# Weight quadrants on the queue of GpSimd, and TensorE in program order within the gate and up products

## The chip, the cores and the metric

The kernel runs on one core of one Trainium2 chip. A core has TensorE (PE, the matrix engine), VectorE (DVE), ScalarE (ACT), GpSimd (POOL) and SyncE (SP). Each runs its own list of instructions in order and waits on semaphores where it needs another's result. SP, ACT and POOL can each put transfers on a queue of their own; 16 DMA engines carry them out. The metric is the time of one execution on the device in microseconds; a lower time is better.

## The reference

The reference is one step of a two-layer streaming encoder for 512 new frames (with 16 meta tokens in front) and 32 frames of a running stream, 560 columns in all. Each layer is a feed-forward half step, a mixer (gated linear attention in layer 0, latent attention in layer 1) and another feed-forward half step. Nearly all of what matters here is in the half steps, of which there are four:

```python
def swiglu_half(h, norm_w, w_gate, w_up, w_down):
    hn = rmsnorm(h, norm_w)
    return h + 0.5 * ((jax.nn.silu(hn @ w_gate) * (hn @ w_up)) @ w_down)
```

The model width is 1024 and the inner width 2816. All data are 32-bit floats.

## The kernel before, in words

**Numbers in two parts.** A matmul takes its operands as a high and a low part. `split` (L330) makes them: ACT casts the source to the high part (L331), DVE subtracts that from the source for the low part (L332). `mm` (L370) multiplies high by high (L378), low weight by high (L379) and high weight by low (L381).

**Seven products for eight.** The gate and up products of a half step treat the 1024 rows of a weight block and the 560 columns of the input as two halves each, and replace the eight block products by seven products of sums and differences (a Strassen scheme). For each pair `f` of 128-column blocks of the inner width, `quads` (L435) loads four quadrants of the weights, r11, r12, r21 and r22, into tiles named `fr` (six buffers), by `quadrant` (L354), two transfers of 256 KB each, gate and up. It forms sums of quadrants on DVE (L451) and hands out the seven weight operands in the order r11, r12, r11 + (r21 + r22), r21 + r22, r21 + r11, r22, and r12 plus the third; `whole` (L360) splits each into tiles `whi` and `wlo` (four buffers of each).

**The order of the seven.** `gate_up` (L467) runs them into three pairs of PSUM banks, A, B and C: b11 into A, b21 into C, t6 onto A, t5 into B, t7 onto A, t4 into C, b22 onto B. After each of them `between` may put in pieces of the down product of the group before (`down`, L544; output Y, added to `h` on DVE at L556). `finish` (L493) combines two banks, scales the columns by the norm's reciprocal root, and makes silu(gate) * up.

**The norm's roots** are not ready when a half step starts. `roots` (L402) has PE sum the squares across partitions (six small matmuls, L410), DVE take a reciprocal square root in eleven small steps (`rsqrt`, L422, lines 424 to 432), and, in the function `finish` that it returns, PE spread the result over the partitions (three transposes, L417). In the first `gate_up` of a half step the program has `roots(0)` between b21 and t6, the first use of its result (L417) after t5, then `roots(1)`, and its L417 behind t7. In the very first half step (`lazy`) `roots(0)` comes after t6.

**Stages.** `ffn` (L562) runs a half step: five groups of `f`, of 2, 4, 4, 4 and 8 blocks, each with its down product; that of the last group runs after the others, alone. In it, and in the last projection of a mixer, the input operands of the next half step are made, and the weights of its first two products are loaded ahead into tiles `raw` (`first_weights`, L348, with `quadrant` too). The other weights are loaded by `load` (L334, transfer at L341) into `raw` (two buffers).

**What sets the order.** A planner (the tile framework) sets the order of each engine's list: it walks through the program with a model of the costs and gives an engine, when it is free, the earliest instruction of the program that is ready in the model. So an engine's list may differ from the order in which the program names its instructions. A `manual_schedule` block holds the engines named to the order of the program for the instructions inside it; the others, and where the block's instructions fall among those outside, stay the planner's. Once set, an engine's list is followed in order on the chip, waits included; so are the queues. All weights are transferred by SP's queue.

Of the kernel before, what the change touches and what calls it, by code (L numbers as in the profile page):

```python
# [52 lines left out]
def weight_plan():  # L53
# [3 lines left out]
    def ffn(i, l):  # L57
        for gi, (f0, f1) in enumerate(GROUPS):
# [3 lines left out]
            for m in range(ND):  # L62
                plan.append((("d", i, l, gi, m), f1 - f0))

    ffn(1, 0)
    for h in range(GH):
        plan.extend((("v", h, j), nk * V_COLS[h] / P) for j, nk in enumerate(V_PARTS[h]))
# [4 lines left out]
        if h >= 2:  # L72
            plan.extend((("go", h - 2, c), 8) for c in range(4))
    ffn(2, 0)
    ffn(1, 1)
    for m in range(6):
        plan.append((("wd", m), 8))
# [212 lines left out]
class Net:  # L290
# [61 lines left out]
        return self.whole(raw)  # L352

    def quadrant(self, t, i, l, f, q):  # L354
        for j, x in enumerate("gu"):
            off, n = PLAN[x, i, l, f + q // 2]
            src = self.a["W"][off:off + P * n].rearrange("(p k c) -> p k c", p=P, k=2)[:, q % 2]
            self.nc.sync.dma_start(t[:, 512 * j:512 * j + 512], src)

    def whole(self, src):  # L360
        hi = self.w.tile([P, 8, P], F32R, name="whi", tag="whi")
# [200 lines left out]
    def ffn(self, i, l, xs, halves, side, turn):  # L562


        ap, fw = Pools(self.tc, side), Pools(self.tc, side)
        acp = ap(f"act{i}{l}")
        if xs.lazy:
            free = [acp.tile([P, 2, T // 2], F32, name="xt", tag=f"a{x}{j}") for j in range(4, 8) for x in "hl"]
            xs.tmp = [t[:, k, :] for t in free for k in range(2)]
        raws, tp = fw(f"raw{i}{l}", 6), fw(f"tmp{i}{l}", 1)  # L570
        fill = []
        last = len(GROUPS) - 1
        for gi, (f0, f1) in enumerate(GROUPS):
            j0 = 4 * (gi % 2) if gi < last else 0
            acts = [(acp.tile([P, T], F32R, name=f"ah{j}", tag=f"ah{j}"),
                     acp.tile([P, T], F32R, name=f"al{j}", tag=f"al{j}")) for j in range(j0, j0 + 4 if gi == last else j0 + f1 - f0)]
            slots = [7 * min((f1 - f0) // 2, 2) - 1]

            def between(k):
                if slots[0] <= 0 or (slots[0] == 7 * min((f1 - f0) // 2, 2) - 1 and k < 2):  # L580
                    return
                for _ in range(-(-len(fill) // slots[0])):
                    fill.pop(0)()
                slots[0] -= 1

            for f in range(f0, f1, 2):
                if gi == last and f == f0 + 4:
                    assert not fill
                    acts += [(acp.tile([P, T], F32R, name=f"ah{j}", tag=f"ah{j}"),
                              acp.tile([P, T], F32R, name=f"al{j}", tag=f"al{j}")) for j in range(4, 8)]  # L590
                self.gate_up(i, l, f, xs, acts[f - f0:f - f0 + 2], raws, tp, between)
            assert not fill
            order = [(m, hf) for m in range(ND) for hf in (0, 1)]
            if gi < last:
                fill = self.down(i, l, gi, acts, halves, order)
        fw.close()
        after = turn()
        order = Quads.ORDER if isinstance(after, Quads) else (
            [(0, 0), (1, 0), (0, 1), (1, 1), (2, 0), (3, 0), (2, 1), (3, 1)] + [(m, hf) for hf in (0, 1) for m in range(4, 8)])
        for f in self.down(i, l, last, acts, halves, order, after):  # L600
            f()
        ap.close()
# [967 lines left out]
```

## Time and profile before

| | us |
|---|---|
| median of three runs | 2117.19 |
| the three runs | 2110.93, 2117.34, 2117.19 |
| the profiled execution | 2109.41 |
| its span, first to last instruction | 2107.5 |
| PE busy | 2026.0 (96%) |
| DVE busy | 1643.2 (78%) |
| ACT busy | 1018.4 (48%) |
| POOL busy | 51.4 (2%) |

In the rows of the profile a group is named by line, engine, operation and output<-inputs, with the tile's shape; "x24" is a count, and a bracket at the end of a timeline's row holds the idle time of the engine before it and what ended that. PE's weight loads (PEld) run beside its matmuls. "SPq" is SP's queue: it issues transfers and waits, and has no busy time. The granted clock is the share of full speed at which PE was allowed to run. The four half steps begin, as PE sees it, at about 0, 679, 1070 and 1707 us.

### The profile page before, as it was taken

To read this page: it belongs to the slowest core of one execution; us is meant where nothing else is said; L and a number is where in the kernel's file an instruction comes from. 1 tells how busy PE (TensorE), PEld (TensorE's weight loads), DVE (VectorE), ACT (ScalarE), POOL (GpSimd) and SP (SyncE) were. 2 spreads that over 40 slices of the span, in tenths; PEclk is the share of its full clock that TensorE was granted. 3 is DMA by queue.
4 is the path that set the end of the run, shared out by engine and by line. 5 is a ranking of instruction groups with operands and counts; after the bars stand their busy time and mean duration, and the time that the engine had idled before them with its cause. 6 is when DMAs were issued, how large, how long until landed. Compare 5 with 4: busy or idle time off the path is not lost.

```text
span 2107.5 us, 38039 instructions
## 1 busy us (share of the span) xinstructions
PE 2026.0 (96%) x15290; PEld 1980.2 (94%) x15290; DVE 1643.2 (78%) x3097; ACT 1018.4 (48%) x1822; POOL 51.4 (2%) x117
## 2 busy tenths in 40 slices
PE   5999999999999899999989999999999979999997
PEld 5999999989999799999979999999988969999997
DVE  8887878556658888788778877886788788878884
ACT  6444445455445444445545444454575454444451
POOL 0000000101110000000000000000210000000000
PEclk8999999999999899999989999999999989999998
DMA  3323222222221332322222322222211223232221
GB/s 131 106 87 107 93 96 78 77 68 71 73 80 55 108 103 82 106 86 91 81 95 96 105 92 91 95 83 92 61 51 59 71 86 100 90 111 91 96 72 62
DMA packets 93633, 183.29 MB, mean 87 GB/s; under 512 B 10433, under 2 KB 22081, under 8 KB 93457
## 3 DMA queue, kind: packets, MB, share of 16 engines
q1 hardware_dynamic: 89632, 176.24, 26.1%
q10 hardware_dynamic: 3824, 4.63, 0.7%
q8 instruction: 120, 1.97, 0.4%
q14 instruction: 57, 0.46, 0.1%
HBM read 176.84 MB, written 3.99 MB: 86 GB/s over the span
## 4 chain that ended last, share of the span: by engine, by line
PE 82%; DVE 10%; ACT 3%; DMA 2%; issue 2%; SPq 0%; POOL 0%; DVEq 0%; ACTq 0%; POOLq 0%
PE Y L381 8%; PE Y L378 8%; PE Y L379 8%; PE A L379 5%; PE A L381 5%; PE A L378 5%; PE ps L378 4%; PE ps L381 4%; PE ps L379 4%; PE B L378 3%; PE B L379 3%; PE B L381 3%; PE C L379 3%; PE C L381 3%; PE C L378 3%; DVE wlo L332 3%
## 5 line engine op out<-in xcount | busy, mean ns | idle before, releaser
L332 DVE TENSOR_TENSOR wlo<-fr,whi 128x1024 fp32r<-128x1024 f32 x302 | 363.9, 1216 | 17.2 <-ACT whi L331 17.0
L378 PE MATMUL Y<-ah,whi 128*128 128x280 f32 (+1 forms) x1408 | 373.8, 291 | 1.9 <-ACT ah L331 1.0
L379 PE MATMUL Y<-ah,wlo 128*128 128x280 f32 (+1 forms) x1408 | 373.4, 292 | 0.0
L331 ACT CAST whi<-fr 128x1024 fp32r<-128x1024 f32 x302 | 313.3, 1049 | 92.9 <-PE C L381 34.6
L378 PE MATMUL A<-x,whi 128*128 128x280 f32 (+1 forms) x1056 | 286.3, 296 | 29.5 <-ACT whi L331 29.5
L379 PE MATMUL A<-x,wlo 128*128 128x280 f32 (+1 forms) x1056 | 285.7, 296 | 1.0 <-DVE wlo L332 1.0
L378 PEld LDWEIGHTS Y<-ah,whi 128*128 128x128 f32 x1408 | 265.2, 188 | 3.4 <-ACT ah L331 1.7
L556 DVE SCALAR_TENSOR_TENSOR h<-Y,h 128x280 f32<-128x280 f32 (+1 forms) x320 | 140.9, 443 | 161.9 <-PE Y L381 161.2
L379 PEld LDWEIGHTS Y<-ah,wlo 128*128 128x128 f32 x1408 | 265.4, 188 | 0.0
L332 DVE TENSOR_TENSOR wlo<-raw,whi 128x512 fp32r<-128x512 f32 (+5 forms) x237 | 203.6, 861 | 76.7 <-ACT whi L331 71.9
L331 ACT CAST whi<-raw 128x512 fp32r<-128x512 f32 (+5 forms) x237 | 176.0, 744 | 173.4 <-PE ps L381 55.2
L381 PE MATMUL Y<-al,whi 128*128 128x280 f32 (+1 forms) x1408 | 233.9, 292 | 0.0
L378 PEld LDWEIGHTS A<-x,whi 128*128 128x128 f32 x1056 | 203.9, 193 | 31.1 <-ACT whi L331 31.1
L451 DVE TENSOR_TENSOR fr<-fr 128x1024 f32<-128x1024 f32 x176 | 214.5, 1219 | 20.4 <-DMA fr<-W 18.1
L379 PEld LDWEIGHTS A<-x,wlo 128*128 128x128 f32 x1056 | 203.7, 193 | 1.7 <-DVE wlo L332 1.4
L381 PEld LDWEIGHTS Y<-al,whi 128*128 128x128 f32 x1408 | 201.2, 189 | 0.0
L378 PE MATMUL B<-x,whi 128*128 128x280 f32 (+1 forms) x704 | 188.6, 293 | 3.4 <-ACT whi L331 3.4
L379 PE MATMUL C<-x,wlo 128*128 128x280 f32 (+1 forms) x704 | 187.1, 292 | 3.5 <-DVE wlo L332 3.5
L379 PE MATMUL B<-x,wlo 128*128 128x280 f32 (+1 forms) x704 | 187.4, 292 | 0.8 <-DVE wlo L332 0.8
L378 PE MATMUL C<-x,whi 128*128 128x280 f32 (+1 forms) x704 | 187.4, 291 | 0.6 <-ACT whi L331 0.6
L381 PE MATMUL A<-x,whi 128*128 128x280 f32 (+1 forms) x1056 | 181.2, 294 | 0.0
L490 ACT COPY r<-A 128x560 f32<-128x560 f32 (+1 forms) x132 | 82.2, 623 | 174.1 <-PE A L381 173.8
(368 smaller groups left out, 4059.2 us busy)
## 6 DMA issues: line engine op xcount, KB each, us to landing
fr<-W SPq DMA_DIRECT2D x352, 256.0 KB, 3.4
raw<-W SPq DMA_DIRECT2D x80, 512.0 KB, 3.5
raw<-W SPq DMA_DIRECT2D x112, 256.0 KB, 2.9
raw<-W SPq DMA_DIRECT2D x40, 128.0 KB, 2.1
h<-xT SPq DMA_DIRECT2D x3, 560.0 KB, 7.6
raw<-W SPq DMA_DIRECT2D x4, 384.0 KB, 3.1
o_y<-h SPq DMA_DIRECT2D x8, 136.0 KB, 2.2
o_y<-h ACTq DMA_DIRECT2D x8, 136.0 KB, 1.9
```

Of the source, the lines that this page charges most:

```text
L331: self.nc.scalar.copy(hi, src)
L332: self.nc.vector.tensor_tensor(lo, src, hi.bitcast(F32), op=ALU.subtract)
L378: f(hi[:, b0 + k, :], xh[:, c], start=not more and k == 0, stop=False)
L379: f(lo[:, b0 + k, :], xh[:, c], start=False, stop=False)
L381: f(hi[:, b0 + k, :], xl[:, c], start=False, stop=k == n - 1)
L451: add = lambda out, x, y: nc.vector.tensor_tensor(out, x, y, op=ALU.add)
L490: nc.scalar.copy(r[:, :, :n], of[:, :, :n])
L556: nc.vector.scalar_tensor_tensor(self.h[:, m, c], Y[:, :n], 0.5, self.h[:, m, c], op0=ALU.mult, op1=ALU.add)
```

## The change

Two things change. `quadrant` puts its transfers on the queue of GpSimd, except those of the very first pair of blocks of the first half step, which stay on SP; this holds for the `fr` tiles and for the first weights of the later half steps, which go into `raw`. And every call of `gate_up` runs inside a block that holds PE to the order of the program. That block includes the pieces of the down product that `between` puts in, and the matmuls of the roots; the planner still sets the order of DVE, ACT, SP and POOL.

```diff
     def quadrant(self, t, i, l, f, q):
+
+        queue = self.nc.sync if (i, l, f) == (1, 0, 0) else self.nc.gpsimd
         for j, x in enumerate("gu"):
             off, n = PLAN[x, i, l, f + q // 2]
             src = self.a["W"][off:off + P * n].rearrange("(p k c) -> p k c", p=P, k=2)[:, q % 2]
-            self.nc.sync.dma_start(t[:, 512 * j:512 * j + 512], src)
+            queue.dma_start(t[:, 512 * j:512 * j + 512], src)
...
-                self.gate_up(i, l, f, xs, acts[f - f0:f - f0 + 2], raws, tp, between)
+                with self.tc.manual_schedule(engines={mybir.EngineType.PE}):
+                    self.gate_up(i, l, f, xs, acts[f - f0:f - f0 + 2], raws, tp, between)
```

## The prediction

> **What bounds the kernel now.** I read the page first, then the busy time by stretches, then the waits of PE, then the timelines around each place where PE stood still.
>
> The head of the page:
>
> ```profile
> span 2107.5 us, 38039 instructions
> PE 2026.0 (96%) x15290; PEld 1980.2 (94%) x15290; DVE 1643.2 (78%) x3097; ACT 1018.4 (48%) x1822; POOL 51.4 (2%) x117
> ```
>
> PE sets the time and has 81 us without work. The waits of PE (total, times, longest) say what ended most of them:
>
> ```profile
> PE A L378 <- ACT whi L331: 29.5, 6, 8.8
> PE Y L417 <- DVE ry L432: 21.4, 8, 3.3
> ```
>
> The view by stretches says where (stretch, length, busy time of PE, PEld, DVE, ACT and POOL with counts, granted clock, DMA share, GB/s):
>
> ```profile
> 0.00:58.00 58.00, 33.09 (x185) 30.72 (x186) 46.88 (x108) 36.62 (x76) 0.20 (x4) 0.85 0.39 128
> 58.00:333.60 275.60, 275.60 (x2141) 275.60 (x2140) 226.57 (x329) 127.44 (x196) 0.00 (x0) 1.00 0.30 97
> 679.00:703.00 24.00, 13.71 (x84) 12.78 (x83) 20.72 (x48) 9.59 (x15) 0.00 (x0) 0.72 0.43 137
> 703.00:775.00 72.00, 71.75 (x557) 71.52 (x556) 61.49 (x93) 35.40 (x58) 0.00 (x0) 1.00 0.31 98
> 1077.00:1095.50 18.50, 8.74 (x44) 7.80 (x43) 14.64 (x34) 5.53 (x8) 0.00 (x0) 0.63 0.19 60
> 1713.00:1734.00 21.00, 8.49 (x38) 7.56 (x38) 15.57 (x35) 6.69 (x9) 0.00 (x0) 0.59 0.53 163
> ```
>
> Inside a feed-forward stage PE has no gap (275.60 of 275.60), so no order of its work and no queue can make that part shorter. What is to be won lies at the four starts of such a stage: idle 24.9 (0 to 58), 10.3, 9.8 and 12.5 us, with the clock down to 0.59 to 0.85. The first start keeps its loads on SP. So the forecast is made at the other three. The second stage's start, on PE, DVE, ACT and SP (start, length, line, form, idle time before it):
>
> ```profile
> 685.12 0.72 PE L410 MATMUL Y<-ones,acc 128*128 128x1 f32 x6
> 688.73 0.54 PE L417 MATMUL Y<-ident,ry 128*128 128x128 f32 x3 [2.88 <-DVE ry L432]
> 689.11 1.19 PE L410 MATMUL Y<-ones,acc 128*128 128x1 f32 x6
> 693.59 0.87 PE L417 MATMUL Y<-ident,ry 128*128 128x128 f32 x3 [3.30 <-DVE ry L432]
> 698.23 0.60 PE L378 MATMUL A<-x,whi 128*128 128x280 f32 x1 [3.76 <-ACT whi L331]
> ...
> 688.51 0.16 DVE L432 SCALAR_TENSOR_TENSOR ry<-rt,ry 128x3 f32<-128x3 f32 x1
> 693.29 0.15 DVE L432 SCALAR_TENSOR_TENSOR ry<-rt,ry 128x3 f32<-128x3 f32 x1
> 693.37 4.99 DVE L451 TENSOR_TENSOR fr<-fr 128x1024 f32<-128x1024 f32 x4
> ...
> 697.13 1.99 ACT L331 CAST whi<-fr 128x1024 fp32r<-128x1024 f32 x2 [2.24 <-DVE fr L451]
> ...
> 679.10 0.80 SPq L358 DMA_DIRECT2D fr<-W  x2
> ...
> SPq L358 <- PE ps L381: 8.9, 1, 8.9
> ```
>
> In program order the third product (t6 into A) comes after the first L410; the first L417 comes after t5 into B; the second L410 after that; the second L417 behind t7. The planner has instead put both root chains ahead of t6, on PE and on DVE. The three additions that t6's weights need (L451) begin when the second chain is over, at 693.37, though the first chain was over at 688.67 (688.51 + 0.16). From their start to t6 are 698.23 - 693.37 = 4.86 us: three additions and a cast. Elsewhere in the stage PE already follows the program (products and pieces alternate whole), so the ordering touches these starts alone.
>
> **The change part by part.** *The queue.* 344 of the 352 loads into fr and the 12 into raw go from SP to POOL's queue. What a load costs there no row shows. From below, SP's issue:
>
> ```profile
> L358 SPq DMA_DIRECT2D fr<-W x352: 327/422/1593, 2.2 to 2006.4; - x176
> fr<-W SPq DMA_DIRECT2D x352, 256.0 KB, 3.4
> ```
>
> 0.42 us is the lower end, SP's longest 1.59 us the upper. POOL's own work on 128 partitions gives the nearest row:
>
> ```profile
> 1502.37 0.99 POOL L1033 TENSOR_TENSOR cos<-cos,yn 128x272 f32<-128x272 f32 x1 [13.39 <-ACT yn L1031]
> ```
>
> I take 1.0 us, which is also the middle of the ends, and keep both for the range. The Trainium skill ("DMA: Bandwidth & Descriptors", Latency and other measured facts) puts the first byte of a transfer issued by GpSimd at about 1 us and of one from SP at about 0.6. By that alone a load would land only 0.4 us later than from SP, the additions of the second and the fourth start would not be held up by it, and the sum would come out some 4 us lower, near 2112; no run here shows it yet.
>
> *The starts.* The eight loads of the four quadrants leave in a burst. The loads of the second and of the fourth stage, as SP issued them:
>
> ```profile
> L358 SPq DMA_DIRECT2D fr<-W x10: 328/430/432, 679.1 to 683.3; - x10
> DMA to landing us min/median/max: 3.3/5.7/6.5
> ...
> L358 SPq DMA_DIRECT2D fr<-W x10: 327/430/500, 1713.7 to 1717.8; - x10
> DMA to landing us min/median/max: 2.9/5.9/6.8
> ```
>
> Second stage: the first of ten lands at 682.4 (679.1 + 3.3), the last at 689.8, 0.82 us apart, the eighth at 688.1. On POOL, issues 1.0 us apart don't queue behind each other: 679.1 + 8 x 1.0 + (3.3 - 0.33) = 690.1. These loads can't start earlier on any queue, since they wait for PE's last projection of the mixer (the 8.9 us of SP's queue for PE ps, L381), which ends at 679.1. PE in program order can't issue the second L410 before t5, so DVE has no second chain to do, and the additions start at the later of 688.67 and 690.1, that is 3.3 us earlier than now. Third stage:
>
> ```profile
> 1077.00 0.72 PE L410 MATMUL Y<-ones,acc 128*128 128x1 f32 x6
> 1079.86 0.16 DVE L432 SCALAR_TENSOR_TENSOR ry<-rt,ry 128x3 f32<-128x3 f32 x1
> 1084.25 1.22 DVE L451 TENSOR_TENSOR fr<-fr 128x1024 f32<-128x1024 f32 x1
> 1089.12 0.60 PE L378 MATMUL A<-x,whi 128*128 128x280 f32 x1 [3.76 <-ACT whi L331]
> ...
> L358 SPq DMA_DIRECT2D fr<-W x10: 328/430/442, 1061.2 to 1065.7; - x10
> ```
>
> Its loads were issued from 1061.2 and are no limit; 1084.25 - 1080.02 = 4.2 us earlier. Fourth stage:
>
> ```profile
> 1723.48 5.00 DVE L451 TENSOR_TENSOR fr<-fr 128x1024 f32<-128x1024 f32 x4
> ```
>
> On POOL the eighth load lands at 1713.7 + 8.0 + (2.9 - 0.33) = 1724.3, so here the additions come 0.8 us later. Together 3.3 + 4.2 - 0.8 = 6.7 us.
>
> Not all of it stays. Both L417 and the second L410 lay in PE's idle time; now they lie between products: 0.38 (688.73 to 689.11) + 0.73 + 0.38 = 1.5 us, three times 4.5. And what is late next is the second L417: in program order it stands between t7 and t4, and t4 is queued behind it. From the second L410 to its L417 it took 693.59 - 689.11 = 4.5 us; t7 covers 3.1 us (a product of 24 matmuls at 71.75 / 557 = 0.129) and L410 0.7, which leaves 0.7 us, three times 2.1 (0 if DVE gives the chain its turn at once, some 10 us if two additions of 1.25 us, 4.99 / 4, get between each time). So the starts bring 6.7 - 4.5 - 2.1 = 0.1 us.
>
> *The first start.* The first quadrants stay on SP, and PE's order there is the program's but for single matmuls pulled ahead while others waited: 0, within 1 us.
>
> *The rest of a stage.* After each start DVE is 85% busy (61.49 of 72) and the split weights are ready just in time. Around 768:
>
> ```profile
> 763.35 2.48 DVE L451 TENSOR_TENSOR fr<-fr 128x1024 f32<-128x1024 f32 x2 [1.97 <-DMA fr<-W]
> 768.68 0.40 PE L379 MATMUL B<-x,wlo 128*128 128x280 f32 x1 [0.25 <-DVE wlo L332]
> ...
> 756.11 1.02 SPq L341 DMA_DIRECT2D raw<-W  x1
> 757.17 2.56 SPq L358 DMA_DIRECT2D fr<-W  x3
> ```
>
> DVE stands 1.97 us for a quadrant there. A pair of loads lands 0.42 + 3.4 = 3.8 us after its start on SP, on POOL 2 x 1.0 + 3.0 = 5.0: 1.2 us more, four stages 4.8. Against it, POOL is not held by the raw load in front (1.02 us). I count half, 2.4 us. Later in a stage weights are far enough ahead to cover this; without that cover each such wait would cost its 1.2 us. At the starts POOL has no other instruction (0.00 (x0) in those stretches), so nothing of its own holds its queue.
>
> **Sum**: 0.1 - 2.4 = 2.3 us slower than the profiled execution, 2109.41 + 2.3 = 2111.7. That execution (span 2107.5, 1.9 around it) lies low among the four known times (2109.41, 2110.93, 2117.19, 2117.34; mean 2113.7). From the mean I get **2116**. A measurement of this kernel can tell about 0.3% (6.3 us) from no change; its own runs differ by as much.
>
> **The rivals.** *A start without a stall.* POOL's queue has no raw loads in front, so in the third stage the quadrants could land while the last projection still runs, and if the planner then does the additions in DVE's gaps before 1077, t6 follows L410 at once: 1089.12 - 1077.73 = 11.4 us, less 1.5, and the work after 1089 no longer runs at half clock (6.3 us of 18.5 at mean clock 0.63), another 3. With the second stage's 1.8, less 2.3 in the fourth and 2.4 in the stages: 10 us, **2104**. For it: DVE had room there (14.64 busy of 18.5). Against it: the loads were on time already at 1061, and the planner still put the additions last.
>
> *DVE starves behind POOL* (the slower side). One mechanism: a load costs POOL 1.3 us or more. Its place is the two gate and up pairs after each start, where two waits of DVE end with a landing, and the starts of stages two and four. At 1.3 a pair lands 2.6 + 3.0 - 3.8 = 1.8 us late, 8 x 1.8 = 14.4; the second start ends at 692.5 (0.9 gained, 2.2 given back), the third gains 2.0, the fourth comes at 1726.7 (3.2 and 2.2 lost): 4.7 more. Together 19, **2133**; at 1.59 about 28. It decides from about 1.1 us on. For it: the weights have no lead there; against it: fr has six buffers, and most loads leave well ahead.
>
> *Nothing that binds is touched.* Data still land after the chains in the planner's view, DVE's order stays and PE only waits elsewhere: **2114**. What SP waited for in a stage were buffers, not its own issuing:
>
> ```profile
> SPq L358 <- DVE wlo L332: 104.1, 24, 9.6
> ```
>
> A second queue frees no buffer. The Trainium skill says this too ("DMA: Bandwidth & Descriptors", Issuing engines are not separate DMA queues): more issuing engines save only issue time, on the same 16 DMA engines. The trace agrees so far (0.42 us an issue).
>
> **How the numbers follow.** Forecast 0.40, the start without a stall 0.22, DVE starved 0.23, nothing touched 0.15. The forecast's own range is 2108 to 2124. The range for 8 in 10 reaches to 2102 for the first rival and to 2134 for the second at 1.3 us. Faster: 0.20 of the first rival and 0.08 of the lower part of the forecast and of the untouched case, 0.28. Slower: 0.21 of the second, 0.08 of the forecast's upper part, 0.29. Same: 0.43.
>
> **What would show it.** At each start: L410, then A's 24 matmuls, B's, and only then L417; L451 right after the first L432 in the third stage, and 5.0 us after L410 in the second (690.1 - 685.12). A gap before the second L417 of about 0.7 us. POOL issues of about 1.0 us and DVE waits on fr that grow by about 1.2 us each. Wrong if PE shows gaps in the middle of a stage, if additions still wait for the second chain, or if a start has no gap at all.

## The result, and the profile after

The changed kernel takes 2130.03 us (median of five runs, 2127.62 to 2135.62) against 2117.34 for the kernel before (five runs beside it, 2110.93 to 2119.69): a ratio of 1.0071, 95% interval 1.0054 to 1.0087. That is slower by 15 us by the ratio (0.0071 x 2117) and by 12.7 us by the medians. The forecast was 2116, no change that can be measured. The profiled execution of the changed kernel is its median, 2130.03; that of before, 2109.41, was one of its fastest, so the two traces lie 20.5 us apart, and every difference below is read against a second trace of before as well.

The page of the changed kernel: its head, the groups of the loads and of the additions (line numbers behind `quadrant` are two higher than before: L378 is L380, L410 is L412, L417 is L419, L432 is L434, L451 is L453).

```profile
span 2128.0 us, 38103 instructions
PE 2029.6 (95%) x15290; PEld 1982.7 (93%) x15290; DVE 1642.5 (77%) x3097; ACT 1018.6 (48%) x1822; POOL 241.2 (11%) x473
...
L360 POOL DMA_DIRECT2D fr<-W x344 | 183.0, 537 | 1198.4 <-DVE wlo L332 879.5
...
L453 DVE TENSOR_TENSOR fr<-fr 128x1024 f32<-128x1024 f32 x176 | 214.8, 1221 | 39.7 <-DMA fr<-W 38.6
...
fr<-W POOLq DMA_DIRECT2D x344, 256.0 KB, 3.7
```

A load costs POOL 0.54 us (537 ns), and lands 3.7 us after its issue (medians); on SP it was 0.42 and 3.4. DVE's work is the same, but its additions wait 39 us for landings. The waits of PE (total, times, longest):

```profile
PE A L380 <- ACT whi L331: 47.0, 5, 15.5
PE Y L419 <- DVE ry L434: 12.1, 6, 3.8
...
PE A L380 <- DVE gu L499: 4.8, 3, 1.6
```

The wait for the transposes has shrunk from 21.4 to 12.1 us and that for t6's weights has grown from 29.5 to 47.0: they are one stretch of time, which now has one wait where it had three. New is a wait of bank A for DVE (L499), 1.6 us in each of three starts. The stretches that answer to those of before, shifted by as much as each stage starts later (columns as there):

```profile
684.50:708.50 24.00, 15.18 (x100) 14.78 (x99) 18.75 (x35) 9.51 (x13) 8.48 (x16) 0.79 0.53 176
708.50:780.50 72.00, 68.34 (x528) 67.54 (x527) 61.98 (x104) 34.81 (x59) 9.59 (x18) 1.00 0.26 85
1086.10:1104.60 18.50, 10.58 (x62) 10.19 (x60) 13.76 (x22) 5.75 (x7) 3.55 (x7) 0.72 0.27 86
1724.60:1745.60 21.00, 4.74 (x22) 4.35 (x22) 12.62 (x21) 3.89 (x4) 8.34 (x16) 0.61 0.48 154
```

In the second and third start PE does more than before (15.18 against 13.71, 10.58 against 8.74), in the fourth less (4.74 against 8.49). And in the 72 us behind the second start, where PE had been busy for 71.75, it now stands still for 3.7. So what was gained at a start was lost right behind it. The second start, from PE's timeline and DVE's, and behind it a row from further on in the stage and two of the third start, from PE's:

```profile
690.78 0.72 PE L412 MATMUL Y<-ones,acc 128*128 128x1 f32 x6
699.61 0.60 PE L380 MATMUL A<-x,whi 128*128 128x280 f32 x1 [8.10 <-ACT whi L331]
...
714.83 0.39 PE L380 MATMUL A<-x,whi 128*128 128x280 f32 x1 [1.59 <-DVE gu L499]
...
719.63 0.54 PE L419 MATMUL Y<-ident,ry 128*128 128x128 f32 x3 [1.46 <-DVE ry L434]
...
694.11 0.16 DVE L434 SCALAR_TENSOR_TENSOR ry<-rt,ry 128x3 f32<-128x3 f32 x1
694.73 2.48 DVE L453 TENSOR_TENSOR fr<-fr 128x1024 f32<-128x1024 f32 x2 [0.46 <-DMA fr<-W]
...
775.99 0.40 PE L381 MATMUL B<-x,wlo 128*128 128x280 f32 x1 [0.61 <-DVE wlo L332]
...
1086.10 0.72 PE L412 MATMUL Y<-ones,acc 128*128 128x1 f32 x6
1094.02 0.60 PE L380 MATMUL A<-x,whi 128*128 128x280 f32 x1 [7.20 <-ACT whi L331]
```

The additions now follow the first root chain (694.11, 694.73), and t6 begins 8.1 us behind the last L412 instead of 12. Then two stalls: one of 1.59 us at 714.83, where the first product of the *next* pair, which the planner has put ahead of the second L419 and of t4, waits until DVE has read bank A; and one of 1.46 us at 719.63 for the second chain.

For the whole of a start I use two spans from PE's timelines: from b21's end to t6's start, and from there to the start of the 22nd product (the fourth pair's first, 772.5 before and 779.8 after in stage two). In us, second, third and fourth stage:

| kernel | stage 2 | stage 3 | stage 4 |
|---|---|---|---|
| before | 12.9 + 74.3 | 12.0 + 75.0 | 15.5 + 72.8 |
| before, profiled again | 13.4 + 74.7 | 12.8 + 73.6 | 15.4 + 73.1 |
| after | 8.7 + 80.2 | 7.8 + 80.8 | 16.1 + 79.3 |

Four to five us are won ahead of t6 in stages two and three and 5.5 to 7 lost behind it; in stage four there is only the loss.

### The profile page after: what moved, and what is told of

Its sections match the earlier page's. It is cut to its first block, busy times and chain, and to the rows that moved or that the text cites. A ratio compares the mean times of both kernels' runs of the same rounds, so it can differ in the third digit from the quotient of the medians.

```text
span 2128.0 us, 38103 instructions
## 1 busy us (share of the span) xinstructions
PE 2029.6 (95%) x15290; PEld 1982.7 (93%) x15290; DVE 1642.5 (77%) x3097; ACT 1018.6 (48%) x1822; POOL 241.2 (11%) x473
## 4 chain that ended last, share of the span: by engine, by line
PE 75%; DVE 13%; DMA 4%; issue 3%; ACT 3%; POOL 1%; SPq 0%; DVEq 0%; ACTq 0%; POOLq 0%
PE Y L383 8%; PE Y L380 8%; PE Y L381 8%; PE A L381 5%; PE A L383 5%; PE A L380 5%; DVE wlo L332 4%; PE ps L380 4%; PE ps L383 3%; PE ps L381 3%; DMA fr<-W 3%; PE C L381 3%; PE C L380 3%; PE C L383 3%; PE B L381 3%
## 5 line engine op out<-in xcount | busy, mean ns | idle before, releaser
L380 PE MATMUL Y<-ah,whi 128*128 128x280 f32 (+1 forms) x1408 | 374.6, 292 | 4.5 <-ACT ah L331 3.7
L380 PE MATMUL A<-x,whi 128*128 128x280 f32 (+1 forms) x1056 | 289.1, 298 | 52.3 <-ACT whi L331 47.0
L360 POOL DMA_DIRECT2D fr<-W x344 | 183.0, 537 | 1198.4 <-DVE wlo L332 879.5
L380 PEld LDWEIGHTS Y<-ah,whi 128*128 128x128 f32 x1408 | 266.0, 189 | 5.8 <-ACT ah L331 4.6
L332 DVE TENSOR_TENSOR wlo<-raw,whi 128x512 fp32r<-128x512 f32 (+5 forms) x237 | 203.6, 860 | 79.5 <-ACT whi L331 74.7
L380 PEld LDWEIGHTS A<-x,whi 128*128 128x128 f32 x1056 | 205.1, 194 | 54.1 <-ACT whi L331 47.5
L453 DVE TENSOR_TENSOR fr<-fr 128x1024 f32<-128x1024 f32 x176 | 214.8, 1221 | 39.7 <-DMA fr<-W 38.6
L380 PE MATMUL C<-x,whi 128*128 128x280 f32 (+1 forms) x704 | 188.9, 293 | 0.0
L380 PE MATMUL B<-x,whi 128*128 128x280 f32 (+1 forms) x704 | 186.5, 290 | 0.0
```

The lines of the kernel that those rows point to most:

```text
L332: self.nc.vector.tensor_tensor(lo, src, hi.bitcast(F32), op=ALU.subtract)
L360: queue.dma_start(t[:, 512 * j:512 * j + 512], src)
L380: f(hi[:, b0 + k, :], xh[:, c], start=not more and k == 0, stop=False)
L453: add = lambda out, x, y: nc.vector.tensor_tensor(out, x, y, op=ALU.add)
```

## The experiments

The theory after the comparison: PE's order loses what it wins because DVE's second root chain comes late, and POOL's queue costs something of its own. Rivals: the loss is all POOL's (later landings), or it lies in the first start, where POOL's loads for the second pair go out beside SP's first ones. The ratios below are to runs of before taken in the same set, with a 95% interval; 0.001 is 2.1 us.

**The kernel before again.**

> The kernel before, unchanged, to see how far two sets of runs of one kernel lie apart and what its profiled execution shows when it is not a low one. Every theory expects a ratio of 1.000 within 0.002 and, for the profile, 2109 to 2120 us. If the profiled execution is again near 2109 and the timed ones near 2117, part of the 20.5 us between the two profiles is how an execution falls, and the 12.7 us between the medians are what has to be explained.

Measured: ratio 0.9991 (0.9979 to 1.0004); its profiled execution took 2110.41. So two sets of runs of one kernel agree within 0.2%, and the profile of before is a usual one, at the fast end of the 2107 to 2123 us that all runs of before but one take in the later sets.

**Each part by itself.** The queue alone (the `manual_schedule` block taken out):

> Only the queue is changed: quadrants on POOL's queue, PE left to the planner. Theory 1 (the loss is PE's program order behind t6): within 3 us of before, about 2119, since additions still wait for the second root chain, and the first stage's start is some 1 us late. Theory 2 (the loss is POOL's queue: later landings, DVE waits of 39 in place of 18 us): most of the 12.7 us, about 2128. Theory 3 (the first start, where POOL's loads for the next pair are issued ahead of SP's first quadrants): about 2122, with the first stage 3 to 5 us longer and the others unchanged.

The order alone:

```diff
-        queue = self.nc.sync if (i, l, f) == (1, 0, 0) else self.nc.gpsimd
+        queue = self.nc.sync
```

> Only PE's program order is changed, all quadrants stay on SP. Theory 1: about 2128, slower by 8 to 12 us: t6 earlier by about 4 us in the second and third stage, but the eighth product behind it later again by 6 us, in the fourth stage with nothing won before. Theory 2: no slower than before, about 2117 or less, with DVE waits on fr back at 18 us. Theory 3: about 2125, the first stage no longer than before but for its stall of 3.8 us ahead of L419.

Measured: queue alone 1.0025 (1.0012 to 1.0037), 5.3 us; order alone 1.0051 (1.0034 to 1.0068), 10.8 us. The two sum to 16 us, the change cost 15: within the intervals, two terms that add. The rival that all is POOL's queue falls. My own first theory's "within 3 us" for the queue is missed too, though the lower end of the interval, 2.5 us, is within it. The rival of the first start expected the first stage to be 3 to 5 us longer with the queue alone. It isn't: the mixer behind it begins on PE at 413.8 us, against 411.5 and 412.6 in the two traces of before. In the order's trace the spans are 8.6 + 79.6, 7.8 + 79.8 and 16.2 + 79.2 us, those of the changed kernel, without POOL.

**The second L419 moved back.** The order alone, and the end of the second half's first `finish` (what needs the second L419) emitted behind b22:

```diff
-        finish(1, 1, A, p5, "neg")
+        e11 = finish(1, 1, A, p5, "neg", first)
...
         product(B, "b22", True)
+        if first:
+            e11()
```

Here `finish` with its last argument true does its first step, which reads the bank, and returns the rest (L503 on) as a function.

> PE's program order, all quadrants on SP, and in the first pair of a stage the last part of the second half's finish (what needs the second L419) is emitted behind t4 and b22, so that the second L419 no longer stands right behind t7. Theory 1: the stalls of 1.5 us ahead of the second L419 and of 1.6 us ahead of the next pair's first product go, 3 x 3.1 us and some 2 us in the first stage, so about 11 us faster than with the order alone: about 2117, and 4 us earlier at t6 of the second and third stage. Theory 2 and 3: as the order alone, within 3 us.

Measured: 0.9997 (0.9981 to 1.0013), 11.4 us faster than the order alone (0.0054 x 2115), as the theory had it. Spans: 8.4 + 76.0, 7.8 + 76.2, 15.8 + 75.9. The second part has come down by 3 to 4 us in each stage; no wait for L419 is left in stages two to four.

**The order in some stages alone.** A block that holds PE only where it is asked for, without and with the moved L419:

```diff
-                with self.tc.manual_schedule(engines={mybir.EngineType.PE}):
+                with self.tc.manual_schedule(engines={mybir.EngineType.PE}) if (i, l) in ((2, 0), (1, 1)) else ExitStack():
```

> PE's program order in the second and third stage alone, its second L419 in its old place, all quadrants on SP. Theory 1: in these two stages the gain at t6 and the loss behind it nearly cancel (0.5 and 0.9 us lost by the profiles with the order alone), so within 2 us of before, ratio 1.000 to 1.001; the 10.8 us of the order alone then lie in stage four (7) and stage one (2 to 3). Rival (each stage loses alike): 5 us slower, ratio 1.0025.

> All quadrants on SP; PE's program order and the late second L419 of the run before, but in the second and third stage alone, the first and fourth left to the planner. Theory 1 (the additions of stages two and three come 4 us earlier, and what was given back behind t6 is the stall at the second L419, cured here; in stages one and four the loads decide, and there the order only gives back): faster than before by 3 us a stage, 6 us in all, about 2109 where before is 2115, ratio 0.997; from b21's end to the 22nd product 84 us in stages two and three against 87, and 88 in stage four. Rival (what is won at t6 is always lost again to weights that come no earlier): ratio 1.000, 87 us.

And in the fourth stage, `(i, l) == (2, 1)`, alone:

> PE's program order in the fourth stage alone, all quadrants on SP. Theory (there the additions wait for the loads, so the order wins nothing ahead of t6 and gives back all that follows): 7 us slower than before, ratio 1.0033, with 95 us from b21's end to the 22nd product against 88. Rival (most of the order's 10.8 us lies in the first stage): within 3 us of before.

Measured: order in stages two and three 1.0000 (0.9988 to 1.0012); the same with the L419 moved **0.9970** (0.9955 to 0.9985), 2109.61 against 2115.85, faster than both kernels; order in stage four 1.0043 (1.0029 to 1.0057), 9 us, with 15.2 + 79.6 us there, as the theory had it. So nearly all of the order's 10.8 us is stage four. In stages two and three a gain and a loss cancel, and with the loss cured the gain shows, 6 us as expected. The fastest of these, PE's timeline of its second start:

```profile
687.43 0.72 PE L412 MATMUL Y<-ones,acc 128*128 128x1 f32 x6
695.89 0.60 PE L380 MATMUL A<-x,whi 128*128 128x280 f32 x1 [7.74 <-ACT whi L331]
...
705.54 0.49 PE L419 MATMUL Y<-ident,ry 128*128 128x128 f32 x3
705.86 0.73 PE L412 MATMUL Y<-ones,acc 128*128 128x1 f32 x6
...
717.59 0.54 PE L419 MATMUL Y<-ident,ry 128*128 128x128 f32 x3
```

Neither L419 has a bracket: PE waits for none of them. The second stands 11.7 us behind its L412 and still nothing waits, since t7, t4, b22 and part of the next product lie between.

Why stage four has nothing to win, from the changed kernel's trace:

```profile
1724.40 0.72 PE L412 MATMUL Y<-ones,acc 128*128 128x1 f32 x6
1740.66 0.60 PE L380 MATMUL A<-x,whi 128*128 128x272 f32 x1 [15.53 <-ACT whi L331]
...
1735.78 1.23 DVE L453 TENSOR_TENSOR fr<-fr 128x1024 f32<-128x1024 f32 x1 [7.52 <-DMA fr<-W]
```

The additions stand 7.52 us for landings. That is not POOL's doing: in the run with the order in stage four alone, all loads on SP, they stand 6.72 us. Both root chains fitted into that time before, at no cost. In program order the second one does not.

**What makes the second L419 late.** The order in the fourth stage, as one block over all pairs instead of one for each, so that the next pair's product can't go ahead of L419:

```diff
+        strict = ExitStack()
+        if (i, l) == (2, 1):
+            strict.enter_context(self.tc.manual_schedule(engines={mybir.EngineType.PE}))
         for gi, (f0, f1) in enumerate(GROUPS):
...
+        strict.close()
         fw.close()
```

> PE's program order in the fourth stage alone, but as one region over all pairs, so that the next pair's first product no longer goes ahead of the second L419 and of t4. Theory (what is late is DVE's second root chain, whose eleven small steps lie between additions and splits of 1.2 us; the product pulled ahead only fills part of that wait): the wait ahead of the second L419 grows to some 6 us, and the kernel is 3 us slower than with the order in the fourth stage alone, ratio about 1.0057. Rival (the product pulled ahead, which waits 1.5 us for bank A, is itself the loss): 1.5 us faster, ratio 1.0036.

Measured: 1.0059 (1.0038 to 1.0080). The times of the two overlap; the trace decides:

```profile
1756.32 0.87 PE L419 MATMUL Y<-ident,ry 128*128 128x128 f32 x3 [6.48 <-DVE ry L434]
```

One wait of 6.48 us in place of two (1.46 and 1.85 in the trace with a block for each pair), and 82.6 us from t6 to the 22nd product instead of 79.6. The product pulled ahead was no loss but filled half of the wait. What is late is the chain, and DVE's timeline of the changed kernel in the same stage shows why (the second L412 stands at 1750.23 on PE):

```profile
1751.35 0.15 DVE L426 TENSOR_SCALAR rv<-Y 128x3 f32<-128x3 f32 x1
1751.42 0.71 DVE L503 TENSOR_TENSOR gu<-gu,yn 128x544 f32<-128x544 f32 x1
1752.06 0.16 DVE L427 TENSOR_SCALAR ry<-rv 128x3 int32<-128x3 int32 x1
1752.13 1.21 DVE L453 TENSOR_TENSOR fr<-fr 128x1024 f32<-128x1024 f32 x1
1753.26 0.15 DVE L432 TENSOR_TENSOR rt<-ry 128x3 f32<-128x3 f32 x1
1753.33 1.22 DVE L332 TENSOR_TENSOR wlo<-fr,whi 128x1024 fp32r<-128x1024 f32 x1
1754.47 0.43 DVE L506 TENSOR_TENSOR gu<-gu 128x272 f32<-128x272 f32 x1
1754.82 0.15 DVE L433 TENSOR_TENSOR rt<-rt,rv 128x3 f32<-128x3 f32 x1
...
1760.47 0.16 DVE L434 SCALAR_TENSOR_TENSOR ry<-rt,ry 128x3 f32<-128x3 f32 x1
```

Eleven steps of 0.15 us take from 1751.35 to 1760.63, 9.3 us, because an addition, a split or a scaling stands between nearly every two of them. The first chain, with DVE to itself, took 2.1 us in stage two (692.15 to 694.27).

**The moved L419 in the changed kernel.**

> The changed kernel with the last part of the second half's finish emitted behind t4 and b22 in the first pair of each stage, so that the second L419 has two more products ahead of it. Theory (the order's cost is the stall there, the queue's cost is a term of its own, and they add): 10 us faster than the changed kernel, 5 us slower than before, ratio 1.0025, about 2120. Rival (POOL's late loads make the stalls, so that the two compound): 1.005 or more.

Measured: 1.0037 (1.0022 to 1.0051), 7.8 us above before. The expected 1.0025 and the queue's own 5.3 us lie in the interval, the 1.005 of the rival at its edge: the order's loss is mostly cured here too, and what is left is about the queue's. The rival isn't excluded by this run alone.

**Where the queue costs.** PE left to the planner, POOL's queue for the first two pairs of each stage alone (`f < 4`), or for the others alone:

> PE left to the planner; POOL's queue for the quadrants of the first two pairs of each stage alone (but the very first), SP for all others. If the queue's cost is what the prediction said, weights that come just in time in the two pairs behind each start: all of the 5 us measured with the queue alone, about 1.0025. Rival (it is spread over the stages, by waits of POOL with no cause shown, and by pieces that come late at a stage's end): within 2 us of before.

> PE left to the planner; SP's queue for the quadrants of the first two pairs of each stage, POOL's for all others. If the queue's cost lies in the two pairs behind each start: as before within 2 us. Rival (spread over the stages): 3 to 5 us slower, about 1.002.

Measured: first two pairs 1.0006 (0.9994 to 1.0018), the others 1.0017 (1.0004 to 1.0029). By the middle values the larger part, 3.6 of 4.9 us, is not where the prediction put it, but the intervals overlap. The waits of DVE for landings, of the second trace of before, of the two, and of the queue alone, in this order:

```profile
DVE fr L451 <- DMA fr<-W: 15.1, 13, 1.8
```

```profile
DVE fr L453 <- DMA fr<-W: 17.4, 16, 2.1
```

```profile
DVE fr L453 <- DMA fr<-W: 31.4, 23, 3.2
```

```profile
DVE fr L453 <- DMA fr<-W: 30.9, 25, 3.3
```

Nearly all of the growth of DVE's waits is in the later pairs. One of these waits and what it does to PE, from DVE's and PE's timelines with the queue alone; in the second trace of before DVE waits 1.40 us there, and PE not at all:

```profile
766.69 2.49 DVE L453 TENSOR_TENSOR fr<-fr 128x1024 f32<-128x1024 f32 x2 [3.04 <-DMA fr<-W]
...
772.02 0.40 PE L381 MATMUL B<-x,wlo 128*128 128x280 f32 x1 [1.33 <-DVE wlo L332]
```

Ahead of this wait POOL had paused for 2.49 us between two loads (the rows are in the last section). With POOL's queue for the later pairs alone, the same loads are on POOL too, but the pause falls at another place, at 872.14 us. DVE and PE at the place shown above, then POOL's pause:

```profile
766.72 2.49 DVE L453 TENSOR_TENSOR fr<-fr 128x1024 f32<-128x1024 f32 x2 [1.95 <-DMA fr<-W]
...
772.05 0.40 PE L381 MATMUL B<-x,wlo 128*128 128x280 f32 x1 [0.24 <-DVE wlo L332]
...
872.14 0.55 POOL L360 DMA_DIRECT2D fr<-W  x1 [2.49 <-issue]
```

So of the 1.33 us of PE some 1.1 go with the pause, and 0.24 are there without it. All waits of this kind on PE with the queue alone (total, times, longest; 0.3 us, once, in the second trace of before):

```profile
PE B L381 <- DVE wlo L332: 2.3, 3, 1.3
```

They account for 2 of the 5.3 us. The time without work on PE grew by 4.3 us in all (82.8 to 87.1), and no run ties the rest to the queue. Three things make a load on POOL later. One that waits for its buffer starts 0.28 us after the release, where SP starts 0.02 us after it (medians of the 141 loads of the trace with the queue alone, and of the 91 of before, whose release the trace shows). The issue takes 0.54 us instead of 0.42, and the landing 3.7 instead of 3.4.

Whether it is the landing or something of POOL's own was tried with the lead of the loads: seven buffers `fr` in place of six, then five, each on POOL and on SP. With seven, PE's list is the same on both queues, and DVE's but for 2 of its 3097 places; with five they differ in a few places.

```diff
-        raws, tp = fw(f"raw{i}{l}", 6), fw(f"tmp{i}{l}", 1)
+        raws, tp = fw(f"raw{i}{l}", 7), fw(f"tmp{i}{l}", 1)
```

> POOL's queue alone, PE left to the planner, and seven buffers fr in place of six, so that loads can leave earlier. Theory (the queue's 5 us are loads that land too late for DVE because their buffer came free just in time): the difference from the same kernel on SP goes to under 2 us, ratios alike within 0.001. Rival (the cost is POOL's own and has nothing to do with the lead of the loads): 4 to 5 us slower than the same kernel on SP.

> The kernel before with seven buffers fr in place of six, all on SP, to compare the run before this one with. If weights are late nowhere in the kernel before: ratio 1.000 within 0.001. If its DVE waits on fr (15 to 18 us) still reach PE: 2 to 4 us faster, 0.998 to 0.999.

> POOL's queue alone with five buffers fr in place of six, so that every load leaves later. Theory (the queue's cost is the later landing of loads whose buffer came free just in time): against the same kernel on SP it loses more than the 5 us seen with six buffers, 10 us or more (ratios 0.005 apart). Rival (POOL's own cost, whatever the lead): 5 us, ratios 0.0025 apart.

> The kernel before with five buffers fr, all on SP, to compare the run before this one with. Both theories: slower than before, by how much they do not say; its DVE waits on fr are longer than the 15 to 18 us with six buffers.

Measured, POOL and SP: seven buffers 1.0014 (0.9998 to 1.0030) and 1.0008 (0.9995 to 1.0022); five 1.0029 (1.0015 to 1.0044) and 0.9987 (0.9974 to 0.9999). So the queue costs 1.3 us with seven (0.0006 x 2115), 5.3 with six and 8.9 with five. The order is that of a cost by late landing: under 2 us with seven, as that theory had it, and with five between its "10 us or more" and the rival's 5. But neighbouring values overlap within their intervals, each of some 3 us to both sides, and POOL's pauses are there with seven buffers too, so this supports the theory and doesn't show it. That SP with five buffers would be slower was a miss of both theories; more on it at the end.

## Why the prediction was wrong

The measured 15 us are 2.3 predicted and some 13 not. By its own steps:

- **PE bounds, and only the starts matter**: half right. As far as the spans show, the order's cost is at starts, but the prediction named gaps in the middle of a stage as a sign against it, and there are some: 0.61 us at 775.99 in the changed kernel, 1.33 us at 772.02 with the queue alone.
- **The additions 3.3 and 4.2 us earlier, in stage four 0.8 later**: right. From b21's end to t6 it is 4.2, 4.2 and -0.6 us (12.9 to 8.7, 12.0 to 7.8, 15.5 to 16.1). In stage two it is more than predicted because a load took 0.54 us and not 1.0: the additions begin 3.95 us behind L412 (690.78, 694.73), where 5.0 was said.
- **Given back, 1.5 + 0.7 us a start**: this is **the step that failed**, a term mis-sized. Behind t6 each start loses 5.9, 5.8 and 6.5 us, 18 in all where 6.6 were counted. The mechanism was named: t4 queued behind the second L419, and DVE's turn as the unknown. The duration was taken from before, where the chain had DVE nearly to itself: 4.5 us from L410 to L417. Beside the additions it is 10.4 (1750.23 to 1760.68). The same sentence had the other bound, "some 10 us" for three starts where additions get between; they got between nearly every two steps. Of the second start's 5.9 us, the roots in PE's path are 1.2, where 1.5 were counted; the waits ahead of L419 and of the product pulled in front of it are 3.1 (1.46 + 1.59), where 0.7 was counted; 0.72 is t6's own wait for its low part, which B's first matmul had half covered before (0.35 was left), and 0.61 is the gap at 775.99, neither of them in the sum. The moved L419 shows the size of the second: without those waits the loss behind t6 is 1.3 to 2.6 us in stages two and three (76.0 and 76.2 against 73.6 to 75.0), near the 2.2 counted. So the starts bring 4.2 + 4.2 - 0.6 - 18 = -10 us where the sum had +0.1, and the order alone cost 10.8.
- **The queue, 2.4 us by loads of 1.0 us each**: right in sign, half the size, and by another way. The issue is 0.54 us, nearest to the bound from SP's row and not to the middle that I took. So it holds up the additions of the second start by 0.46 us only, and the rival of a starved DVE does not come by its price of 1.3 us; that its 2133 lies near the measured 2130 is luck. By the middle values most of the cost lies in the later pairs, of which the prediction said that weights are far enough ahead. DVE's waits for landings say that they are not: 15.1 us became 30.9, nearly all in those pairs. That these waits are the whole of the 5.3 us is not shown. The Trainium skill ("DMA: Bandwidth & Descriptors", Latency and other measured facts) puts a first byte at about 1 us from GpSimd and at about 0.6 us from SP, which by estimate is 0.4 us later. The 3.7 against 3.4 us here agree with it.
- **Base**: 2113.7 was good; later sets of before have medians of 2114.6 to 2115.9, the five runs beside the changed kernel 2117.34.

Of the rivals, "a start without a stall" and "nothing that binds is touched" fell with the changed trace: the third start still has 7.2 us ahead of t6, and DVE's order did change. The chance of 0.29 for slower was meant for POOL; two thirds of the slowing came from PE's order.

What stays open: the queue's cost by pairs and by buffers is read from intervals that overlap, and PE's waits for late weights in its trace add up to less than half of it. The 1.1 us that PE waits for `ah` ahead of the last group's down products of stage two with the queue alone (0.2 in the second trace of before) wasn't followed to its start; in stage one it is the other way round (0.2 against 1.1), so it may be no effect of the queue.

## What to carry to other kernels

A chain of tiny instructions costs its own few microseconds only on an idle engine: before moving it beside bulk work, count the bulk instructions that its steps will stand behind, one for each step (here 2.1 us became 9.3). Holding an engine to program order pays only where the program has the slack in the right place; look which start waits for data and which for the chain, and do it in the latter alone, with the consumer two products later. And a load that leaves when its buffer comes free has no lead, so that a few tenths of a microsecond of a slower queue reach the engine that waits for it (here DVE's waits doubled); how much of that reaches the engine that bounds the kernel has to be measured.

## What the runs showed of the hardware beside that

POOL stood for 2.49 us between the two loads of one quadrant, with nothing shown that it waited for. The queue alone, then the changed kernel:

```profile
760.93 1.60 POOL L360 DMA_DIRECT2D fr<-W  x3 [2.49 <-issue]
...
1215.35 1.59 POOL L360 DMA_DIRECT2D fr<-W  x3 [2.49 <-issue]
...
1903.31 0.54 POOL L360 DMA_DIRECT2D fr<-W  x1 [2.48 <-issue]
```

```profile
765.63 1.60 POOL L360 DMA_DIRECT2D fr<-W  x3 [2.49 <-issue]
```

All other issues are even (minimum, median and maximum of the changed kernel):

```profile
L360 POOL DMA_DIRECT2D fr<-W x344: 536/536/677, 1.3 to 2026.5; - x172
```

The pause goes with the count of transfers and not with the place: it stands ahead of the 114th, the 220th and the 326th transfer that POOL issues (those into `raw` counted), 106 apart, in each of the traces that get so far, with five, six and seven buffers. With the later pairs alone on POOL the 114th and the 220th fall at 872.14 and 1762.24 us, and with the first two pairs alone, 68 transfers, there is none. The first pause stands ahead of the wait of 3.04 us of DVE at 766.69 and of PE's gap at 772.02, shown above. Its cause wasn't found.

The granted clock changes the length of a stage from one execution to another. Between 18 and 64 us it was 0.81 in some traces and 0.70 in others, with the same code in the first stage (the second trace of before, then the order in stages two and three):

```profile
18.00:64.00 46.00, 30.55 (x183) 28.50 (x183) 41.50 (x93) 26.54 (x56) 0.00 (x0) 0.81 0.14 50
```

```profile
18.00:64.00 46.00, 31.27 (x159) 29.44 (x158) 38.49 (x90) 24.65 (x52) 0.00 (x0) 0.70 0.15 49
```

PE did 24 matmuls fewer in the same time, some 3 us. With the changed kernel the mixer behind the first stage begins on PE at 416.4 us, 4 to 5 us later than in the traces of before (411.5 and 412.6). With the order in stages two and three, whose first stage is that of before, it begins at 415.9. So most of this can be the clock, and no cost of the change can be read from it.

With five buffers on SP, the third stage has no stall at its start at all. From PE's timeline, then the last of the additions for it, from DVE's:

```profile
1089.70 0.72 PE L410 MATMUL Y<-ones,acc 128*128 128x1 f32 x6
1090.29 0.38 PE L378 MATMUL B<-x,whi 128*128 128x280 f32 x1
...
1043.12 1.22 DVE L451 TENSOR_TENSOR fr<-fr 128x1024 f32<-128x1024 f32 x1
```

The planner, with fewer buffers, put the additions 46 us ahead of that start, into the down product before. In the fourth stage, too, the time from b21's end to t6 fell, from 15.5 to 6.4 us, and PE's wait ahead of L417 fell to 3.6 us in all. But products then wait for low parts, most of them in the middle of a stage (12.7 us in 15 waits), so that only 0.13% is left of the gain (0.9987). This is the prediction's start without a stall, reached by a setting that takes a buffer away: as the loads had been issued 16 us ahead of the start before (1061.2, 1077.0), what was missing at this start was a place for the additions in DVE's list, not data.
